# Weight halves in tiles of 1024 columns, a reordered boundary, and a gate block moved ahead in a two-layer gMLP and forgetting-attention kernel

## The chip, the cores and the metric

The kernel runs on one core of a Trainium2 chip. TensorE (PE) multiplies, VectorE (DVE) and ScalarE (ACT) do elementwise work, GpSimd (POOL) does a few small operations, and SyncE (SP) issues most transfers. Each engine runs its instructions in order; semaphores join them. The metric is the device time of one execution in microseconds; lower is better.

## The reference

A model of 1024 features over 512 tokens, with 256 memory rows. Layer A is a gMLP block with four heads of attention on the memory; layer B attends with forget gates (12 heads of 64) and again on the memory. Each layer ends in a feed-forward network of 2816 hidden columns. RMS norms stand before and behind every block:

```python
a = rmsnorm(h, ln_mix_pre[layer])
# layer A: u, v, q_mem = split(a @ w_in_a)
main = gelu(u) * (tril(w_s) @ layernorm(gelu(v)) + b_s)      # per chunk of 128 tokens, 6 groups
# layer B: q, q_mem = split(a @ w_in_b); k, v, log_f from s_in @ w_shared_kv
main = softmax(q k^T / 8 + c_t - c_s, causal) v              # c = cumsum(log_f)
mem_out = memory_attention(q_mem, mem_n, w_mem_kv)           # 4 heads of 64, 256 rows
h = h + rmsnorm(concat(main, mem_out) @ w_out, ln_mix_post)
f = rmsnorm(h, ln_ffn_pre)
h = h + rmsnorm((silu(f @ w_gate) * (f @ w_up)) @ w_down, ln_ffn_post)
```

All is in fp32.

## The kernel before

**Number form.** Every fp32 operand of a matrix product is kept as two tiles, hi and lo, of a faster type (fp32r). `split` (L240) makes them: ScalarE copies `hi`, VectorE subtracts `lo = src - hi`. `mm3` (L191 to 195) then does three products, hi times hi, hi times lo, lo times hi. So each weight goes: transfer of 512 KB to a `raw` tile (128 x 1024, four buffers, SP's queue), two splits of 512 columns, and the products. The halves lie in eight slots of 512 columns for `hi` and eight for `lo` (`pair_of_parts`, L133). In rows of the profile these are `whi<-raw` on ACT and `wlo<-raw,whi` on DVE.

**The order.** A scheduler sets each engine's order from the order of the code, from priorities (`high_priority` lets a block go first) and from explicit order constraints (`issue_after`, and `behind`, L249, which does it for several instructions). What a slot, PSUM buffer or `raw` buffer holds must be released before the next user starts.

**Layer A** (`layer_a`, L565). Tokens and query weights are loaded and multiplied first (`query_weights`, `tokens`). The input's norm ends in a sum (`st`), `var` on VectorE, a power on GpSimd (`rsqrt`, L262), and a broadcast on TensorE (`rb`, L259): `Norm.finish` (L281) is the first part, `spread` (L298) the second. The memory's norm (`var_2`, `rb_2`) goes the same way; then keys and values of the memory are made (`mem_project`) and four heads attend to it (`attend`, with `mp`, `tr`, `mo`). `fill` is a queue of pieces of value work (24: three blocks of eight), each 12 matmuls of 256 columns. `pieces(n)` puts n of them ahead of the next step, and `attend` takes the remaining sixteen between its heads. Behind the attend, `gate_inputs(m)` (L680) makes the gate columns u for one group, `stats` and `normed` the layer norm of v, and `spatial` multiplies with the spatial weights (`rows` and `s` are its products).

**The boundary** (L857) joins a block's output projection to the next block's input. `tail(tb)` (L772) ends one quarter of the tokens: it adds the product to y, squares it with a running sum on ScalarE (L793), adds the sum (L795), takes the power on GpSimd, and scales y (L814). `turn(half, pairs)` transposes y on TensorE (`yt`, L821), adds it to the residual h (L826), scales and splits the next input (`hs`, `xs`), and squares it (`nnorm.pair`, L314). `group` runs the first products of the next block while the second half is being turned; `nnorm.finish` and `spread` (rb_3 and rb_4 at the first FFN boundary) give the scale to `evac`.

**The FFN** (L1042). Gate and up products run as `Seven` (L947): a Strassen-like scheme of seven products of 12 matmuls of 256 columns on sums of weight blocks, in the order 1, 7, 2, 6, 4, 3, 5. `sums` adds the blocks in `raw` on VectorE; each product splits its own 512-column block. `end` adds the products (L1008 to L1011), and the rows are gated. In the first pair of an FFN products 1, 2, 3 of both come first. 40 Sevens run in all. The down products (`moving_pair`, `y`) stream through the same slots. `combined` (L923) makes the input's sums.

**The end.** `give` (L1329) turns, adds and stores the last tokens; the last quarter is stored in four pieces, alternating on SP's and ACT's queue.

## Time and profile before

| | |
|---|---|
| median of three runs | 1121.44 us (1121.39 to 1121.47) |
| the profiled execution | 1121.42 us |
| its span, first to last instruction | 1119.7 us |
| granted TensorE clock, mean | 0.999 |
| PE, PEld, DVE, ACT, POOL busy | 1107.3, 1002.7, 892.0, 660.3, 28.5 us |

The span leaves out 1.72 us around the first and the last instruction. A row of a timeline gives start and duration in us, engine, line, operation, output and inputs, shapes, the count of instructions put together (x), and in brackets the idle time before with what ended it. A row of a group gives busy time and the mean ns of one. A row of waits gives total, times and the longest. A row with only a time, a duration and a name is a piece of the chain of waits that ended last. Matmuls are pipelined: one of 256 columns shows 0.28 us, but the next starts before it has ended.

### The profile page before, as it was taken

How to read it: one execution, taken by the hardware profiler on the slowest of the kernel's cores; microseconds unless marked ns; L12 is line 12 of the kernel's file. 1: busy time of each engine (PE TensorE's matmuls, PEld its weight loads, DVE VectorE, ACT ScalarE, POOL GpSimd, SP SyncE). 2: the span in 40 equal slices, each digit the busy share in tenths (PEclk: the TensorE clock that was granted, in tenths of full speed). 3: DMA queues.
4: the chain of work that ended last, by engine and by line, in shares of the span. 5: the costliest groups of instructions: out<-in, count | busy, mean ns of one | idle time of the engine just before them, and what ended most of it. 6: DMA issues, size and time to landing. Idle time of an engine off the chain costs nothing.

```text
span 1119.7 us, 19536 instructions
## 1 busy us (share of the span) xinstructions
PE 1107.3 (99%) x7409; PEld 1002.7 (90%) x7409; DVE 892.0 (80%) x1721; ACT 660.3 (59%) x1388; POOL 28.5 (3%) x41
## 2 busy tenths in 40 slices
PE   8999999999999999999999999999999999999998
PEld 6998889999899899998988898889999899899996
DVE  7979448999598578796968889958998598588776
ACT  7775458755266255476757677768765266255453
POOL 0100001000000000001000000001000000000000
PEclk9999999999999999999999999999999999999999
DMA  7413231334224234244242655421235234233222
GB/s 265 151 49 109 77 97 58 100 108 151 76 89 140 74 99 127 76 135 148 63 128 59 153 128 137 135 76 57 65 106 152 74 101 133 70 109 118 76 76 76
DMA packets 63557, 118.12 MB, mean 105 GB/s; under 512 B 5164, under 2 KB 39992, under 8 KB 63464
## 3 DMA queue, kind: packets, MB, share of 16 engines
q1 hardware_dynamic: 62584, 116.05, 33.8%
q8 instruction: 58, 0.95, 0.4%
q0 software_dynamic: 192, 0.52, 0.2%
q10 hardware_dynamic: 688, 0.31, 0.1%
q14 instruction: 35, 0.29, 0.1%
HBM read 104.71 MB, written 2.10 MB: 95 GB/s over the span
## 4 chain that ended last, share of the span: by engine, by line
PE 86%; DVE 7%; ACT 3%; issue 2%; POOL 1%; DMA 1%; SPq 0%; POOLq 0%; DVEq 0%; ACTq 0%
PE y L193 9%; PE y L195 9%; PE y L194 9%; PE a L194 5%; PE a L193 5%; PE a L195 5%; PE ps L195 3%; PE ps L194 3%; PE ps L193 3%; PE e L193 3%; PE e L194 3%; PE x L194 3%; PE x L193 3%; PE x L195 3%; PE e L195 3%; DVE wlo L241 2%
## 5 line engine op out<-in xcount | busy, mean ns | idle before, releaser
L241 ACT CAST whi<-raw 128x512 fp32r<-128x512 f32 x460 | 276.2, 620 | 267.0 <-PE y L195 118.6
L241 DVE TENSOR_TENSOR wlo<-raw,whi 128x512 fp32r<-128x512 f32 x460 | 305.2, 685 | 108.8 <-ACT whi L241 106.6
L193 PE MATMUL y<-whi,fhi 128*128 128x512 f32 (+1 forms) x356 | 140.0, 394 | 0.0
L194 PE MATMUL y<-wlo,fhi 128*128 128x512 f32 (+1 forms) x356 | 139.4, 392 | 0.0
L195 PE MATMUL y<-whi,flo 128*128 128x512 f32 (+1 forms) x356 | 139.4, 392 | 0.0
L194 PE MATMUL a<-xslo,whi 128*128 128x256 f32 x320 | 90.0, 281 | 0.0
L194 PE MATMUL x<-xslo,whi 128*128 128x256 f32 x320 | 89.9, 281 | 0.0
L195 PE MATMUL x<-xshi,wlo 128*128 128x256 f32 x320 | 89.9, 281 | 0.0
L193 PE MATMUL x<-xshi,whi 128*128 128x256 f32 x320 | 89.8, 281 | 0.0
L193 PE MATMUL a<-xshi,whi 128*128 128x256 f32 x320 | 89.8, 281 | 0.0
L195 PE MATMUL a<-xshi,wlo 128*128 128x256 f32 x320 | 89.8, 281 | 0.0
L193 PEld LDWEIGHTS y<-whi,fhi 128*128 128x128 f32 x356 | 66.9, 188 | 15.7 <-ACT fhi L241 0.7
L195 PEld LDWEIGHTS y<-whi,flo 128*128 128x128 f32 x356 | 66.9, 188 | 15.5 <-DVE flo L241 0.2
L194 PEld LDWEIGHTS y<-wlo,fhi 128*128 128x128 f32 x356 | 67.0, 188 | 14.7 <-DVE wlo L241 0.2
L193 PE MATMUL ps<-xshi,whi 128*128 128x256 f32 (+1 forms) x224 | 67.5, 304 | 0.0
L195 PE MATMUL ps<-xshi,wlo 128*128 128x256 f32 (+1 forms) x224 | 67.1, 302 | 0.1
L194 PE MATMUL ps<-xslo,whi 128*128 128x256 f32 (+1 forms) x224 | 66.4, 299 | 0.0
L193 PEld LDWEIGHTS a<-xshi,whi 128*128 128x128 f32 x320 | 60.4, 189 | 0.4
L194 PEld LDWEIGHTS a<-xslo,whi 128*128 128x128 f32 x320 | 60.3, 188 | 0.3
L193 PEld LDWEIGHTS x<-xshi,whi 128*128 128x128 f32 x320 | 60.4, 189 | 0.0
L195 PEld LDWEIGHTS x<-xshi,wlo 128*128 128x128 f32 x320 | 60.3, 189 | 0.0
L194 PEld LDWEIGHTS x<-xslo,whi 128*128 128x128 f32 x320 | 60.3, 188 | 0.0
(283 smaller groups left out, 3091.1 us busy)
## 6 DMA issues: line engine op xcount, KB each, us to landing
raw<-in_w_gate SPq DMA_DIRECT2D x44, 512.0 KB, 3.6
raw<-in_w_up SPq DMA_DIRECT2D x44, 512.0 KB, 3.5
raw<-in_w_down SPq DMA_DIRECT2D x44, 512.0 KB, 4.0
raw<-in_w_out SPq DMA_DIRECT2D x16, 512.0 KB, 4.5
raw<-in_w_b_q SPq DMA_DIRECT2D x8, 512.0 KB, 3.5
raw<-in_w_a_v SPq DMA_DIRECT2D x6, 512.0 KB, 7.0
raw<-in_w_a_u SPq DMA_DIRECT2D x6, 512.0 KB
raw<-in_w_v SPq DMA_DIRECT2D x6, 512.0 KB, 3.7
```

Of the source, the lines that this page charges most:

```text
L193: PE.matmul(o, w[0], x[0], start=start, stop=False, skip_group_check=more)
L194: PE.matmul(o, w[0], x[1], start=False, stop=False, skip_group_check=more)
L195: return PE.matmul(o, w[1], x[0], start=False, stop=stop, skip_group_check=more)
L241: last_parts[:] = A.copy(hi, src), (eng or V).tensor_sub(lo, src, hi)
```

## The change

Six things change.

1. The hi and lo tiles become four slots of 1024 columns each. `columns` cuts them. Most splits stay 512 wide, within one slot; but the Sevens' pairs (1,2), (6,3) and (5,4), the gate weights `w_a_u` and the FFN's down weights in its middle groups (`whole`) are split by one instruction of 1024 columns per engine. Product 7 takes a slot by itself. In layer B a query and a key share one slot.
2. The second query weight is loaded as two halves of 256 KB; the feature blocks 1 to 3 of x are issued behind its first half.
3. In layer A twelve value pieces, formerly eight, stand ahead of the memory's projection, and its key weights are loaded later. The attend's filler is then twelve value pieces and the four pieces of a `gate_block(0)`; `gate_inputs(0)` behind the attend is gone. Its GELU goes with the values'.
4. `var` and the power in `Norm.finish` get high priority.
5. At a boundary the last quarter's square and sum (`chain`) stand ahead of the squares of the first half's turned pairs 2 and 3; the second half's squares are made behind `evac`; `combined` stands behind the last turned parts.
6. The last tail has high priority as the others do; `give_last` scales feature blocks 0 to 3 on ScalarE and adds two at a time on VectorE, turns into another PSUM tag for them, and issues all four stores on SP.

TensorE does the same matmuls as before. VectorE's rows fall from 1667 to 1475 and ScalarE's from 1262 to 1061, as the compiled order counts them with neighbours of one line and tile put together.

In the orders below a name's number tells instances apart; a row is line, operation, output and inputs, and the output's shape. The first place is VectorE at the memory norm: `mparts` are the memory's lo parts, `var` the sum plus epsilon. Before:

```order
L246 SCALAR_TENSOR_TENSOR mparts_402<-mem_329,gains,mparts_402 128x256
L246 SCALAR_TENSOR_TENSOR mparts_405<-mem_329,gains,mparts_405 128x256
L241 TENSOR_TENSOR wlo_411<-raw_408,whi_410 128x512
L241 TENSOR_TENSOR wlo_415<-raw_408,whi_414 128x512
L241 TENSOR_TENSOR wlo_421<-raw_418,whi_420 128x512
L241 TENSOR_TENSOR wlo_425<-raw_418,whi_424 128x512
L292 TENSOR_SCALAR var_433<-st_428 128x2
```

Now:

```order
L251 SCALAR_TENSOR_TENSOR mparts_420<-mem_319,gains,mparts_420 128x256
L251 SCALAR_TENSOR_TENSOR mparts_423<-mem_319,gains,mparts_423 128x256
L298 TENSOR_SCALAR var_449<-st_444 128x2
L251 SCALAR_TENSOR_TENSOR mparts_426<-mem_320,gains,mparts_426 128x256
L251 SCALAR_TENSOR_TENSOR mparts_429<-mem_320,gains,mparts_429 128x256
```

`var` has moved ahead of the weight splits and of most memory parts. TensorE has 60 matmuls between `st` and `rb` here, where 48 stood.

The second place is TensorE at the first FFN boundary, where the last quarter's y is first turned (`yt`) between products of the next block (`ps`). Before:

```order
L193 MATMUL ps_2056<-xshi_1940,whi_2036 128x256
L194 MATMUL ps_2056<-xslo_1941,whi_2036 128x256
L821 MATMUL yt_2106<-ident,y_1652 128x128
L193 MATMUL ps_2054<-xshi_1989,whi_1880 128x256
L194 MATMUL ps_2054<-xslo_1990,whi_1880 128x256
L821 MATMUL yt_2106<-ident,y_1667 128x128
```

Now:

```order
L198 MATMUL ps_1987<-xshi_1891,whi_1971 128x256
L199 MATMUL ps_1987<-xslo_1892,whi_1971 128x256
L200 MATMUL ps_1987<-xshi_1891,wlo_1972 128x256
L848 MATMUL yt_2037<-ident,y_1595 128x128
L848 MATMUL yt_2037<-ident,y_1610 128x128
```

The turns of the two quarters (y_1652 and y_1667 before, y_1595 and y_1610 now) stand together, behind 36 products since the turn before, where 26 stood.

The third place is VectorE in a steady Seven of the first FFN (`e`, `a`, `x` are its PSUM products, `s` its sums). Before:

```order
L1008 TENSOR_TENSOR s_3_2794<-e_2792,s_3_2794 128x256
L974 TENSOR_TENSOR raw_2923<-raw_2925,raw_2923 128x512
L241 TENSOR_TENSOR wlo_2959<-s_4_2932,whi_2958 128x512
L975 TENSOR_TENSOR raw_2923<-raw_2923 128x512
L241 TENSOR_TENSOR wlo_2988<-raw_2923,whi_2987 128x512
L241 TENSOR_TENSOR wlo_3005<-raw_2925,whi_3004 128x512
L1009 TENSOR_TENSOR s_3_2794<-a_2791,s_3_2794 128x256
L1011 TENSOR_TENSOR s_3_2793<-x_2790,s_3_2793 128x512
L1063 TENSOR_TENSOR s_3_2794<-s_3_2794,rbc 128x512
L1063 TENSOR_TENSOR s_3_2793<-s_3_2793,rbc 128x512
L241 TENSOR_TENSOR wlo_3021<-raw_2923,whi_3020 128x512
L241 TENSOR_TENSOR wlo_3037<-raw_2925,whi_3036 128x512
```

Now:

```order
L1013 TENSOR_TENSOR raw_2947<-raw_2947 128x512
L246 TENSOR_TENSOR wlo_2875<-raw_2814,whi_2874 128x1024
L1054 TENSOR_TENSOR s_3_2697<-a_2694,s_3_2697 128x256
L1056 TENSOR_TENSOR s_3_2696<-x_2693,s_3_2696 128x512
L1108 TENSOR_TENSOR s_3_2697<-s_3_2697,rbc 128x512
L1108 TENSOR_TENSOR s_3_2696<-s_3_2696,rbc 128x512
L246 TENSOR_TENSOR wlo_2892<-raw_2816,whi_2891 128x1024
```

Two splits of 512 around the last sums have become one of 1024 ahead of them, for (6,3), and one behind them, for (5,4).

The diff, cut to its core:

```diff
--- before.py
+++ after.py
@@ -130,11 +130,12 @@
-    def pair_of_parts(n=512, aside=False):
-        if aside:
-            return act("whi"), act("wlo")
-        return (wp.tile([P, max(n, 512)], F32R, tag="hi", name=name("whi"), bufs=8)[:, :n],
-                wp.tile([P, max(n, 512)], F32R, tag="lo", name=name("wlo"), bufs=8)[:, :n])
+    def pair_of_parts(n=1024):
...
+        return [wp.tile([P, max(n, 1024)], F32R, tag=t, name=name(f"w{t}"), bufs=4)[:, :n] for t in ("hi", "lo")]
...
+    def columns(pair, c0, c1):
+        return [t[:, c0:c1] for t in pair]
@@ -146,32 +147,36 @@
-    def prepared(src, shape, eng=None):
+    def prepared(src, shape, step=512):
...
-        return weight_parts(raw, shape, eng)
...
-    def weight_parts(raw, shape, eng=None):
+        return weight_parts(raw, shape, step)
...
+    def weight_parts(raw, shape, step=512):
...
-        parts = []
-        for d in range(0, n, 512):
-            pair = pair_of_parts(min(512, n - d))
-            split(raw[:, d : min(d + 512, n)], *pair, eng)
-            parts += cut(pair, shape[1])
-        return parts
...
-    def moving_pair(src, aside=False):
+        pair = pair_of_parts(n)
+        for c in range(0, n, step):
+            at = c, min(c + step, n)
+            split(raw[:, at[0] : at[1]], *columns(pair, *at))
+        return cut(pair, shape[1])
...
+    def moving_pair(src, aside=False, whole=False):
...
+        pair = [] if aside else pair_of_parts()
+        if whole:
+            split(four, *(t.rearrange("p (k m c) -> p m k c", m=4, k=2) for t in pair))
...
-            hi, lo = (t.rearrange("p (m c) -> p m c", m=4) for t in pair_of_parts(aside=aside))
-            split(four[:, :, x, :], hi, lo)
+            both = (act("whi"), act("wlo")) if aside else columns(pair, 512 * x, 512 * x + 512)
+            hi, lo = (t.rearrange("p (m c) -> p m c", m=4) for t in both)
+            if not whole:
+                split(four[:, :, x, :], hi, lo)
@@ -289,8 +294,9 @@
-            V.tensor_scalar_add(v[:, t0:t1], st[:, t0:t1], RMS_EPS)
-            rsqrt(self.r4[:, t0:t1], v[:, t0:t1], t1 - t0)
+            with tc.high_priority():
+                V.tensor_scalar_add(v[:, t0:t1], st[:, t0:t1], RMS_EPS)
+                rsqrt(self.r4[:, t0:t1], v[:, t0:t1], t1 - t0)
@@ -582,10 +588,12 @@
-        query_weights(1, 0, 1024)
-        tokens(1, 2)
-        tokens(2, 4)
+        query_weights(1, 0, 512)
+        with tc.issue_after(last_load[0].ins):
+            tokens(1, 2)
+            tokens(2, 4)
...
+        query_weights(1, 512, 1024)
@@ -620,7 +628,27 @@
-            fill = queue([value_block(j) for j in range(3)])
+            us, wu = [], []
...
+            def gate_block(m):
...
+                o = []
...
+                def load():
+                    wu.append(prepared(i["w_a_u"][m], (KT, P), 1024))
...
+                def piece(n):
+                    if n == 0:
+                        o.append(ps("mm", s="u"))
+                    for k in range(2 * n, 2 * n + 2):
+                        mm3(o[0], wu[m][k], a[k], k == 0, k == KT - 1)
+                    if n == 3:
+                        us.append(plain("u"))
+                        V.tensor_mul(us[m], o[0], rbc)
...
+                return load, [lambda n=n: piece(n) for n in range(4)]
...
+            fill = queue([value_block(j) for j in range(3)] + [gate_block(0)])
@@ -645,11 +673,11 @@
-            pieces(1)
+            pieces(3)
...
+            norm.finish((0, NMEM))
...
-            norm.finish((0, NMEM))
-            pieces(3)
+            pieces(5)
@@ -659,7 +687,7 @@
-                for vt in vg.values():
+                for vt in (*vg.values(), us[0]):
@@ -721,7 +747,6 @@
-            gate_inputs(0)
@@ -765,7 +790,7 @@
-            return tc.high_priority() if tb == TB - 1 and not last else ExitStack()
+            return tc.high_priority() if tb == TB - 1 else ExitStack()
@@ -881,7 +908,12 @@
-                nnorm.pair(j, cols)
+                if sums:
+                    nnorm.pair(j, cols)
...
+        def second_turn():
+            turn(1, range(2, 4), False)
+            turned_parts.extend(last_parts)
@@ -896,14 +929,19 @@
-        tail(3, lambda: turn(0, (2,)))
-        turn(0, (3,))
+        tail(3, lambda: turn(0, (2,), False))
+        with behind(chain):
+            nnorm.pair(2, h0)
+        turn(0, (3,), False)
+        with behind(chain):
+            nnorm.pair(3, h0)
...
-                     after={3: lambda: turn(1, range(2)), 5: lambda: turn(1, range(2, 4)),
-                            6: lambda: nnorm.finish(h0)})
+                     after={3: lambda: turn(1, range(2), False), 5: second_turn, 6: lambda: nnorm.finish(h0)})
...
+        for j in range(KT // 2):
+            nnorm.pair(j, h1)
@@ -952,54 +990,61 @@
-            w1, w2 = loaded(src(0)), loaded(src(1))
-            self.a = [w[:, d : d + 512] for w in (w1, w2) for d in (0, 512)]
+            self.raws = loaded(src(0)), loaded(src(1))
+            self.a = [w[:, d : d + 512] for w in self.raws for d in (0, 512)]
...
-        def parts(self, src):
-            pair = pair_of_parts()
+            self.w = {}
...
+        def parts(self, src, *which):
+            n = 512 * len(which)
+            pair = pair_of_parts(n)
...
-            return pair
+            for x, n in enumerate(which):
+                self.w[n] = columns(pair, 512 * x, 512 * x + 512)
...
-            self.w1 = self.parts(a11)
+            self.parts(self.raws[0], 1, 2)
...
-            self.w2 = self.parts(a12)
...
-            for k, w in enumerate(cut(w, P)):
+            for k, w in enumerate(cut(self.w[w], P)):
...
-            a11, a12, a21, a22 = self.a
...
+            if what in (3, 6) and 3 not in self.w:
+                self.parts(self.raws[0], 6, 3)
+            elif what in (4, 5) and 4 not in self.w:
+                self.parts(self.raws[1], 5, 4)
+            elif what == 7:
+                self.parts(self.s3, 7)
...
-                self.product(self.p, self.w1, 0)
+                self.product(self.p, 1, 0)
...
-                self.product(self.x[:, left], self.w2, 2)
+                self.product(self.x[:, left], 2, 2)
...
-                self.product(self.x[:, right], self.parts(a12), 5)
+                self.product(self.x[:, right], 3, 5)
...
-                self.product(self.q, self.parts(a22), 4, True)
+                self.product(self.q, 4, 4, True)
...
-                self.product(self.p, self.parts(a21), 6, True)
+                self.product(self.p, 5, 6, True)
...
-                self.product(self.p, self.parts(a11), 3, True)
+                self.product(self.p, 6, 3, True)
...
-                self.product(self.q, self.parts(self.s3), 1)
+                self.product(self.q, 7, 1)
@@ -1081,10 +1126,11 @@
-        a, close = boundary(phase, G_MIX_POST + layer, G_FFN_PRE + layer, nnorm, rb, first, evac_first, scaled)
+        a, close, turned_parts = boundary(phase, G_MIX_POST + layer, G_FFN_PRE + layer, nnorm, rb, first, evac_first, scaled)
...
-        xs, last = combined(a, scaled, xp)
+        with behind(turned_parts):
+            xs, last = combined(a, scaled, xp)
@@ -1117,7 +1163,7 @@
-                    w = down_weights(layer, k0 + 2 * kp, dh)
+                    w = down_weights(layer, k0 + 2 * kp, dh, whole=True)
@@ -1265,7 +1310,8 @@
-            pair["q"], pair["k"] = pair_of_parts(), pair_of_parts()
+            both = pair_of_parts()
+            pair["q"], pair["k"] = columns(both, 0, 512), columns(both, 512, 1024)
@@ -1326,17 +1372,35 @@
-    def give(tb, order, queues=(nc.sync,)):
+    def give_last(tb):
...
+        c0, c1 = tb * P, (tb + 1) * P
+        at = slice(c0, c1)
+        for k0, k1 in ((4, 6), (0, 2), (6, 8), (2, 4)):
+            tr = ps("tr" if k0 >= 4 else "mm", s="yt")
+            for x, k in enumerate(range(k0, k1)):
+                turned(ys, k, (tb,), tr[:, x * P : (x + 1) * P])
+            if k0 >= 4:
+                for x, k in enumerate(range(k0, k1)):
+                    residual(tr[:, x * P : (x + 1) * P], k, (c0, c1), G_FFN_POST + 1)
+            else:
+                t = temp("g", (P, 2, P))
+                for x, k in enumerate(range(k0, k1)):
+                    A.activation(t[:, x, :], tr[:, x * P : (x + 1) * P], AF.Copy, scale=gain(G_FFN_POST + 1, k))
+                V.tensor_add(h[:, k0:k1, at], h[:, k0:k1, at], t)
+            nc.sync.dma_start(out[:, k0:k1, at], h[:, k0:k1, at])
...
+    def give(tb, order):
...
-        for n, some in enumerate(order):
+        for some in order:
...
-            queues[n % len(queues)].dma_start(out[:, k0:k1, c[0] : c[1]], h[:, k0:k1, c[0] : c[1]])
+            nc.sync.dma_start(out[:, k0:k1, c[0] : c[1]], h[:, k0:k1, c[0] : c[1]])
```

41 lines of the change are left out of this document (21 added, 20 removed).

## The prediction, made before the changed kernel was run

> **What bounds the kernel now.** I read the page first, then what TensorE waits for, then the stretches of time, and at last the timelines around each wait.
>
> ```profile
> span 1119.7 us, 19536 instructions
> PE 1107.3 (99%) x7409; PEld 1002.7 (90%) x7409; DVE 892.0 (80%) x1721; ACT 660.3 (59%) x1388; POOL 28.5 (3%) x41
> ...
> PE rb L259 <- POOL r L262: 2.5, 4, 1.7
> PE yt L821 <- ACT y L814: 1.0, 2, 0.5
> PE ps L193 <- ACT whi L241: 0.7, 1, 0.7
> PE e L193 <- ACT s L1003: 0.4, 1, 0.4
> PE tr L456 <- DVE mp L449: 0.3, 1, 0.3
> ```
>
> TensorE is busy 99% of the span, and the change takes no matrix product away. So its time can only come out of TensorE's waits: 1119.7 - 1107.3 = 12.4 us, ramp and final transfer among them. The list (total, times, longest) says where: the broadcasts of a norm (rb) for a GpSimd power, the turning of y (yt) for ScalarE, and single waits at the start, in the FFN (e) and in attention (tr). VectorE's 80% is an average over unlike stages:
>
> ```profile
> 30.00:60.00 30.00, 27.95 (x233) 27.43 (x233) 26.18 (x58) 21.83 (x52) 3.81 (x2) 1.00 0.47 150
> 160.00:195.00 35.00, 34.31 (x245) 31.57 (x244) 26.82 (x57) 28.81 (x60) 3.80 (x5) 1.00 0.13 39
> 245.00:265.00 20.00, 20.00 (x171) 20.00 (x170) 20.00 (x36) 12.71 (x28) 0.00 (x0) 1.00 0.36 109
> ```
>
> The columns are the stretch, its length, and the busy time of PE, PEld, DVE, ACT, POOL. Layer A has 2.05 us of PE gap in 30; the first boundary 0.69 in 35. In the first FFN's gate and up products VectorE is full, 20.00 of 20, while TensorE is not held up: that cover is thin.
>
> **The first loads.** The second query weight, 512 KB, is first needed at 7.5 us:
>
> ```profile
> 1.75 5.72 DMA raw<-in_w_a_q
> 8.17 0.49 PE L193 MATMUL ps<-ahi,whi 128*128 128x512 f32 x1 [0.69 <-ACT whi L241]
> raw<-in_w_a_q SPq DMA_DIRECT2D x2, 256.0 KB, 3.2
> ```
>
> The 256 KB load issued at 0.81 landed after 3.2 us, at 4.0; 768 KB more (a block of x and this weight) came by 7.47, 3.46 us later. Split in halves, the first leaves 256 KB behind it: 3.46 x 256/768 = 1.15 us earlier. TensorE's wait at 8.17 (0.69, and two idle matmuls in front) goes; the blocks of x that now come later could hold the next steps. I take -0.9, bounds 0 and -1.2.
>
> **The memory norm (var_2, rb_2).** The largest wait:
>
> ```profile
> 31.86 2.49 DVE L241 TENSOR_TENSOR wlo<-raw,whi 128x512 fp32r<-128x512 f32 x4
> 34.27 0.15 DVE L292 TENSOR_SCALAR var<-st 128x2 f32<-128x2 f32 x1
> 34.34 2.48 DVE L241 TENSOR_TENSOR wlo<-raw,whi 128x512 fp32r<-128x512 f32 x4
> 34.49 2.89 POOL L262 TENSOR_TENSOR r<-var,mhalf 128x2 f32<-128x2 f32 x1 [7.56 <-DVE var L292]
> 34.25 0.28 PE L194 MATMUL ps<-mparts,whi 128*128 128x256 f32 x1
> ...
> 35.44 0.28 PE L195 MATMUL ps<-mparts,wlo 128*128 128x256 f32 x1
> 37.44 0.43 PE L259 MATMUL rb<-ident,r 128*128 128x128 f32 x2 [1.73 <-POOL r L262]
> ```
>
> The sum stands on VectorE behind memory parts and four weight splits; the power then takes 2.89 us, beside four more splits (VectorE instructions with two SBUF inputs), though one of this size takes 0.98 elsewhere (187.18 below). The matmul after 35.44 would have started at 35.56, so 1.88 us are lost. After the change var follows two memory parts, and 60 matmuls at 0.119 (34.25 to 35.44 is ten of them) stand between the sums and rb_2, 7.1 us, where 48 stood. The twelve more come from value pieces, which are moved ahead; the memory's key weights go behind the value weights on SP's queue for it, and nothing asks for them before rb_2. Even a power of 2.89 us and a var 1.5 us late fit in. I take -1.9; bounds -1.9 and -0.9 (if half of that lateness is left).
>
> The rest of layer A: the wait on mp (0.3 in the list) loses the splits beside it, but the mem_v split now waits for a 1024-wide slot that the memory products free. I take -0.2, bounds -0.5 and +0.3. The filler of the attend keeps its sixteen pieces of 12 x 0.119 = 1.4 us (a gate piece is six matmuls of 512, as long). But `gate_inputs(0)`, 5.6 us, stood behind the attend and hid GELU, statistics and the normalised v:
>
> ```profile
> 80.03 1.03 PE L456 MATMUL tr<-ident,mp 128*128 128x128 f32 x8
> 89.40 1.31 POOL L262 TENSOR_TENSOR rv<-rv,mhalf 128x4 f32<-128x4 f32 x1 [42.75 <-DVE rv L694]
> 94.45 0.68 DVE L241 TENSOR_TENSOR vlo<-vg,vhi 128x512 fp32r<-128x512 f32 x1
> 100.56 0.27 PE L738 MATMUL rows<-wlo,tri 128*128 128x128 f32 x1
> ```
>
> The spatial products begin behind the last of `rows`, at 100.7; without those 5.6 us at 95.1, and the second vlo is ready at 95.13. The spatial weights' splits now lie ahead, in the attend, and bring that some 1 us earlier. It just fits: +0.3, bounds 0 and +1.0.
>
> **The two FFN boundaries (yt_5, rb_3).**
>
> ```profile
> 174.14 0.61 ACT L241 CAST whi<-raw 128x512 fp32r<-128x512 f32 x1
> 175.40 1.34 ACT L814 ACTIVATE y<-y,r 128x512 f32<-128x512 f32 x2 [0.64 <-POOL r L262]
> 176.17 0.76 PE L821 MATMUL yt<-ident,y 128*128 128x128 f32 x5 [0.51 <-ACT y L814]
> 763.33 1.34 ACT L814 ACTIVATE y<-y,r 128x512 f32<-128x512 f32 x2 [0.64 <-POOL r L262]
> 186.86 0.15 DVE L292 TENSOR_SCALAR var<-st 128x2 f32<-128x2 f32 x1
> 187.18 0.98 POOL L262 TENSOR_TENSOR r<-var,mhalf 128x2 f32<-128x2 f32 x1 [11.82 <-DVE var L292]
> 188.22 0.43 PE L259 MATMUL rb<-ident,r 128*128 128x128 f32 x2 [0.18 <-POOL r L262]
> ```
>
> TensorE stands 0.51 us (0.8 with the broken pitch around it) until y is scaled, at both boundaries. Now 36 products of 256 columns stand between yt_4 and yt_5 instead of 26: ten times 0.119 = 1.2 us more cover, and the chain is no later. The wait goes. Against it, one product's split (wlo) now lies one 512-wide row (0.69) later on VectorE, half of it uncovered by my reading of the order, 0.3. And rb_3 has 8 products behind its sums, not 23. They ended at 188.2 - 23 x 0.119 = 185.5, so var, at 186.86, was 1.4 us late on VectorE. High priority takes that away and 15 x 0.119 = 1.8 of cover goes: +0.4, or nothing if var now comes at once; I take 0. Each boundary -0.8 + 0.3 + 0.0 = -0.5, bounds -0.8 and +0.4, so -1.0 for two. The boundary in front of layer B has the same exchange with smaller waits: -0.2, bounds -0.5 and +0.5.
>
> **The 1024-wide splits.** No row has one. From
>
> ```profile
> L241 DVE TENSOR_TENSOR wlo<-raw,whi 128x512 fp32r<-128x512 f32 x460 | 305.2, 685 | 108.8 <-ACT whi L241 106.6
> L1009 DVE TENSOR_TENSOR s<-a,s 128x256 f32<-128x256 f32 x40 | 16.7, 417 | 2.8 <-ACT s L997 2.7
> 219.12 3.09 DVE L241 TENSOR_TENSOR wlo<-raw,whi 128x512 fp32r<-128x512 f32 x5
> 261.53 1.14 ACT L241 CAST whi<-raw 128x512 fp32r<-128x512 f32 x2
> ```
>
> 256 columns take 0.417 and 512 take 0.685; so 1024, an estimate, 0.685 + 2 x 0.268 = 1.22, bounds 0.685 and 1.37 (once and twice the 512). Five in a row take 3.09, a pitch of (3.09 - 0.685)/4 = 0.60; at such a pitch a 1024 takes 0.60 + 2 x 0.268 = 1.13, so a merged pair saves VectorE 0.07. A gate-up pair of Sevens lasts 14 products of 12 matmuls, 14 x 12 x 0.119 = 19.9 us. VectorE's rows in it were 30 of 512 and 4 of 256 (0.33 apart), 19.3 us; now they are 6 of 1024, 18 of 512 and 4 of 256: 6.8 + 10.8 + 1.3 = 18.9. This is worth the wait at 266 (e on s, 0.4 in the list and 0.2 around it) and nothing more: TensorE is full in the steady Sevens. -0.6, bounds 0 and -0.7.
>
> The price is coarser slots. A Seven now takes all four; each comes free after the second of its two products and is needed again four products later (4 x 1.42 = 5.7 us). ScalarE's half (two of its 512s take 1.14, last row above) and VectorE's 1.13 leave 3.4 us. For the pair (5,4) VectorE has the last sums of the Seven before in front (0.3 + 3 x 0.60, behind a copy of 0.4): 0.4 + 2.1 + 1.1 = 3.6, which leaves 2.1. In the first Sevens of each FFN those sums come on top of `combined`, which now stands behind the turned parts, and the third product waits for a 1024-wide split in place of a 512-wide one. VectorE's rows from the last broadcast to that split are 8.6 us long by the order and these durations, 7.1 before: 1.5 more is the upper bound of a new wait there, and a 1024-wide split's extra length, 1.13 - 0.69 = 0.4, the lower. I take 0.5, since TensorE has the products with hi to do first; twice: +1.0.
>
> **Tail.**
>
> ```profile
> 1113.66 2.75 DVE L826 SCALAR_TENSOR_TENSOR h<-yt,gains,h 128x128 f32<-128x128 f32 x9
> 1115.24 1.58 ACTq L1339 DMA_DIRECT2D out<-h  x2
> 1114.03 2.19 SPq L1339 DMA_DIRECT2D out<-h  x3
> ```
>
> VectorE's nine updates (0.31 apart) end at 1116.4 and the last transfer follows. Four of them become four scalings on ScalarE and two sums of 256 (0.33 apart): two 0.31 saved, and the turns no longer wait for `tr` slots. All four transfers queue on SP, 0.4 apart, which gives part back. -0.4, bounds 0 and -0.6.
>
> Sum: -0.9 - 1.9 - 0.2 + 0.3 - 1.0 - 0.2 - 0.6 + 1.0 - 0.4 = -3.9. Attention in layer B keeps its products; where its query and key pair share one slot I count 0, bounds -0.5 and +1.0. The profiled run's own time is 1121.42 (1.72 more than its span), 0.02 under the median: 1121.4 - 3.9 = **1117.5 us**.
>
> **Rivals.** *The FFNs take it back.* The first Sevens' waits come at 1.5 each, boundaries give nothing, and the wait at 266 stays (VectorE full, 20.00 of 20, speaks for it): -0.9 - 1.9 - 0.2 + 0.3 + 3.0 - 0.4 = -0.1, or 1121.3 at the worst; halfway to the forecast, 1119.4, is its lower end, and 1120.4 its middle. *Slower: VectorE becomes the bound in the Sevens.* If a 1024-wide split holds VectorE for twice a 512's duration, 1.37, six per gate-up pair add 6 x 0.24 = 1.4 to 18.9: 20.3 of 19.9 us. Each of the 20 pairs (40 Sevens) would lose 0.4, +8, about 1125.5. It decides from 1.30 a split ((19.9 - 18.9)/6 + 1.13). The row of 256 against 512 speaks against it, since the slope would have to change. The Trainium skill, "VectorE: DVE Perf Modes", section "The TRN2 errata — SBUF-src ops pay a fixed extra latency per instruction", says that one large tile pays the gap once and many small ones each time; by that rule a merged pair is cheaper, as I took it. *A slow power at the boundaries.* With 8 to 12 products of cover, a power of 2.89 in place of 0.98 at rb_3 and its two likes costs 3 x 1.9 = 5.7, about 1123.2. For it speaks 34.49 above; against it, that only one full-size split stands beside var there, not four. The Trainium skill, "GPSIMD Engine Reference", section "8. Key points", says that GpSimd shares its SBUF interfaces with VectorE and suffers from instructions with two SBUF inputs; the two rows agree. *The change doesn't do what it says*: the order that is compiled leaves every wait where it is, 1121.4. Little speaks for it, since var_2's new place is read from the order itself.
>
> **How the numbers follow.** The forecast has a chance of 0.66, the FFN rival 0.17, VectorE's bound 0.08, the slow power 0.06, no change 0.03. This kernel's measurements tell 0.2% (2.24 us) from no change. Under 1119.2 lie nearly all of the forecast and a sixth of the FFN rival: 0.69. Over 1123.7 lie VectorE's bound and part of the slow power: 0.11. The rest, 0.20, is within. The terms' lower bounds add to -1.2 - 1.9 - 0.5 - 1.6 - 0.5 - 0.7 - 0.6 - 0.5 = -7.5, and the first Sevens' +0.8 makes -6.7; not all come together, so the range begins at -6.4, 1115.0. Its upper end takes in most of the FFN rival, 1120.9.
>
> **What would show it.** rb_2 without a wait on the power; no wait of yt on y at 175 and 763; the query wait at 8 gone; a 1024-wide split near 1.22; in the Sevens no wait of TensorE on wlo or whi. Waits of e or x on a split in every Seven, or rb waits over 1.5 us at the boundaries, would prove me wrong.

## The result, and the profile after

The changed kernel takes 1127.55 us (median; 1126.25 to 1128.53), the kernel before beside it 1121.45: a ratio of 1.0054, 95% interval 1.0041 to 1.0067. It is slower, by 6 us. The forecast was 1117.5, the range 1115.0 to 1120.9, and slower had a chance of 0.11. Times are medians, since a single execution can stray: one of ten of a kernel in the experiments (all splits 512 wide) took 1807.35 us.

The profiled execution took 1126.25 us. Its page begins:

```profile
span 1124.5 us, 19060 instructions
PE 1103.8 (98%) x7408; PEld 998.5 (89%) x7409; DVE 882.3 (78%) x1559; ACT 640.0 (57%) x1232; POOL 28.5 (3%) x41
```

VectorE (DVE) and ScalarE (ACT) have 10 and 20 us less to do than before, and TensorE (PE) is busy 3.5 us less for the same products. The span is nevertheless 4.8 us longer, so TensorE's idle time went from 12.4 to 20.7 us. The list of TensorE's waits (total, times, longest) says for whom:

```profile
PE e L200 <- DVE wlo L246: 2.8, 3, 1.4
PE ps L198 <- ACT whi L246: 2.8, 4, 1.0
PE x L198 <- ACT whi L246: 2.2, 2, 1.1
PE a L198 <- ACT whi L246: 1.6, 4, 0.6
PE rb L264 <- POOL r L267: 1.3, 3, 0.6
...
PE yt L848 <- ACT y L841: 1.1, 2, 0.6
```

The rb wait of 1.7 us is gone from the list, as forecast. New or longer are waits of the Sevens (`e`, `x`, `a`) and of the boundary products (`ps`, 0.80 at each FFN boundary) for split weights. The yt wait, which was to go, stands there as before, and so does the wait for the second query weight: it is 1.02 of the 2.8 us on `ps`, now at 7.06 (before, 0.69 at 8.17). Where the time went is read from the start times of the same products in both traces (kernel after minus kernel before, in us):

| stretch | forecast | measured |
|---|---|---|
| start to the first turning of y (layer A) | -2.7 | -2.80 |
| the two FFN boundaries (first turning of y to the first Seven) | -1.0 | +1.04 and +1.10 |
| first group of each FFN (its first Seven to the first Seven of the next group) | +1.0 | +3.13 and +4.85 |
| the other groups of the first FFN, without its last Sevens | -0.6 for both FFNs | -1.33 |
| the last Sevens of the first FFN | | +1.28 |
| the other groups of the second FFN | | -1.68 |
| boundary before layer B | -0.2 | +0.20 |
| attention of layer B | 0 | -1.11 |
| tail | -0.4 | +0.16 |
| sum | -3.9 | +4.84 |

Three kinds of stretches made the kernel slower: the FFN boundaries, the last Sevens of the first FFN, and above all the first group of each FFN. Here are three stretches of 10 us from the first Seven of the first FFN, before and then after (stretch, length, busy time of PE, PEld, DVE, ACT, POOL, then clock, DMA share and GB/s):

```profile
210.46:220.46 10.00, 10.00 (x86) 10.00 (x85) 8.95 (x18) 7.33 (x15) 0.00 (x0) 1.00 0.07 16
220.46:230.46 10.00, 10.00 (x87) 10.00 (x86) 8.00 (x14) 5.39 (x13) 0.00 (x0) 1.00 0.57 196
230.46:240.46 10.00, 10.00 (x86) 10.00 (x86) 9.98 (x19) 5.39 (x12) 0.00 (x0) 1.00 0.34 107
```

```profile
208.70:218.70 10.00, 8.69 (x69) 8.08 (x68) 8.13 (x14) 4.98 (x8) 0.00 (x0) 1.00 0.31 99
218.70:228.70 10.00, 10.00 (x86) 10.00 (x87) 7.56 (x11) 5.27 (x10) 0.00 (x0) 1.00 0.44 144
228.70:238.70 10.00, 9.00 (x72) 8.40 (x71) 9.97 (x17) 6.69 (x12) 0.00 (x0) 1.00 0.11 26
```

TensorE was never short there; now it loses 1.3 and 1.0 us. VectorE does less in the first two stretches (8.13 and 7.56 of 10) and is full in the third, where TensorE waits. It was not too slow on average; it could not work ahead.

The timeline of that place shows what held it (start, duration, engine; idle time before and its releaser in brackets):

```profile
221.29 0.28 PE L199 MATMUL e<-t3lo,whi 128*128 128x256 f32 x1
221.61 1.05 ACT L246 CAST whi<-raw 128x1024 fp32r<-128x1024 f32 x1 [2.58 <-PE e L199]
222.63 0.69 DVE L1011 TENSOR_TENSOR s<-raw,raw 128x512 f32<-128x512 f32 x1 [2.44 <-DMA raw<-in_w_gate]
223.24 3.49 DVE L246 TENSOR_TENSOR wlo<-raw,whi 128x1024 fp32r<-128x1024 f32 x3
227.58 0.68 DVE L1014 TENSOR_TENSOR raw<-raw,raw 128x512 f32<-128x512 f32 x1
229.71 1.28 DVE L1108 TENSOR_TENSOR s<-s,rbc 128x512 f32<-128x512 f32 x2
233.50 0.69 DVE L1015 TENSOR_TENSOR raw<-raw 128x512 f32<-128x512 f32 x1
234.41 2.94 ACT L246 CAST whi<-raw 128x1024 fp32r<-128x1024 f32 x3
```

ScalarE's cast at 221.61 waits for a product (`e`): no slot is free until TensorE has read one. The `e` that ends just before it is product 7 (its input is `t3`), which holds a whole slot with half of its columns. Then three splits come in one piece at 223.24, two for the first two Sevens and one for the third, and the third Seven's sums fall behind them and behind the end of the two Sevens before. The last of those sums runs at 233.50, the cast that reads it starts at 234.41, behind ScalarE's casts of rows, and TensorE waits at 235.5 to 237.2.

At the boundary, the profile shows the power of y's last quarter (before, it took 0.92 us, from 174.44, and y was scaled at 175.40):

```profile
171.10 0.21 DVE L820 SCALAR_TENSOR_TENSOR v<-ss,rms_eps 128x1 f32<-128x1 f32 x1
171.23 0.68 DVE L246 TENSOR_TENSOR wlo<-raw,whi 128x512 fp32r<-128x512 f32 x1
171.39 2.13 POOL L267 TENSOR_TENSOR r<-v,mhalf 128x1 f32<-128x1 f32 x1 [7.26 <-DVE v L820]
171.83 0.68 DVE L246 TENSOR_TENSOR xslo<-hs,xshi 128x512 fp32r<-128x512 f32 x1
172.43 0.68 DVE L326 TENSOR_TENSOR sq<-sq,sq 128x512 f32<-128x512 f32 x1
173.55 1.33 ACT L841 ACTIVATE y<-y,r 128x512 f32<-128x512 f32 x2 [1.58 <-POOL r L267]
177.29 0.39 PE L198 MATMUL ps<-xshi,whi 128*128 128x256 f32 x1 [0.80 <-ACT whi L246]
```

Counted from the first turning of y (161.60 now, 164.40 before), `v` comes at 9.50 us, 0.25 earlier than before (9.75), but the power takes 2.13 us beside three full-size VectorE instructions. So y is scaled at 11.95, where it was 11.00: 0.95 us later, nearly all of the boundary's +1.04. ScalarE stands idle for 1.58 us in front of that, the next weight casts come behind it, and a boundary product waits for one at 177.29.

### The profile page after: what moved, and what is told of

It reads as the page before. It is cut to its first block, busy times and chain, and to the rows that moved or that the text cites. A ratio compares the mean times of both kernels' runs of the same rounds, so it can differ in the third digit from the quotient of the medians.

```text
span 1124.5 us, 19060 instructions
## 1 busy us (share of the span) xinstructions
PE 1103.8 (98%) x7408; PEld 998.5 (89%) x7409; DVE 882.3 (78%) x1559; ACT 640.0 (57%) x1232; POOL 28.5 (3%) x41
## 4 chain that ended last, share of the span: by engine, by line
PE 84%; DVE 8%; ACT 4%; issue 2%; DMA 1%; POOL 1%; SPq 0%; POOLq 0%; DVEq 0%
PE y L198 9%; PE y L200 9%; PE y L199 9%; PE a L200 4%; PE a L198 4%; PE a L199 4%; PE ps L200 3%; PE ps L199 3%; PE ps L198 3%; PE e L200 3%; PE x L200 3%; PE x L198 3%; PE x L199 3%; PE e L198 3%; PE e L199 3%; DVE wlo L246 2%
## 5 line engine op out<-in xcount | busy, mean ns | idle before, releaser
L246 ACT CAST whi<-raw 128x1024 fp32r<-128x1024 f32 (+1 forms) x302 | 247.6, 844 | 260.5 <-PE y L200 97.5
L246 DVE TENSOR_TENSOR wlo<-raw,whi 128x1024 fp32r<-128x1024 f32 (+1 forms) x302 | 286.5, 969 | 96.0 <-ACT whi L246 94.0
L200 PEld LDWEIGHTS a<-xshi,wlo 128*128 128x128 f32 x320 | 60.4, 189 | 0.0
```

Source lines behind the costliest of these rows:

```text
L200: return PE.matmul(o, w[1], x[0], start=False, stop=stop, skip_group_check=more)
L246: last_parts[:] = A.copy(hi, src), (eng or V).tensor_sub(lo, src, hi)
```

## Experiments

Times are medians beside runs of the kernel before on the same chip; "first groups" are the two first groups of the table. Line numbers differ from kernel to kernel.

**The parts one by one.** The changes of layer A alone, on the kernel before (512-wide slots, old boundary, old end; the norm's sum with high priority stays in):

```diff
-            V.tensor_scalar_add(v[:, t0:t1], st[:, t0:t1], RMS_EPS)
-            rsqrt(self.r4[:, t0:t1], v[:, t0:t1], t1 - t0)
+            with tc.high_priority():
+                V.tensor_scalar_add(v[:, t0:t1], st[:, t0:t1], RMS_EPS)
+                rsqrt(self.r4[:, t0:t1], v[:, t0:t1], t1 - t0)
...
-            pieces(1)
+            pieces(3)
             xs = mem_inputs(0, memt)
-            wk = mem_key_weights(0)
             norm.finish((0, NMEM))
-            pieces(3)
+            wk = mem_key_weights(0)
+            pieces(5)
```

> The kernel before with parts 2, 3 and 4 of the change alone (halved query load, twelve value pieces ahead and the gate block in the attend, high priority for var and the power); slots of 512, old Sevens, old boundary order, old end. Theory L (layer A's gain is real and needs none of the tiles): the start and the memory norm give -2.8 us as in the changed kernel's trace up to the first yt, so 1118.6, and S1 (the first product of the first Seven) comes some 2.8 us earlier than before. Rival (the gain hangs on the four 1024-wide slots): about 1121, yt no earlier. If the priority of var alone disturbs the boundaries, up to +1 on top.

Measured: 1118.28 against 1121.27, ratio 0.9975 (0.9965 to 0.9984). Layer A ends 2.62 us earlier, and each FFN boundary is about 0.5 us shorter (45.43 us for the first, 46.05 before): of these changes only the high priority touches them. So layer A's gain is real and needs no wider tiles.

The tiles alone, on the kernel before:

```diff
-        return (wp.tile([P, max(n, 512)], F32R, tag="hi", name=name("whi"), bufs=8)[:, :n],
-                wp.tile([P, max(n, 512)], F32R, tag="lo", name=name("wlo"), bufs=8)[:, :n])
+        return [wp.tile([P, max(n, 1024)], F32R, tag=t, name=name(f"w{t}"), bufs=4)[:, :n] for t in ("hi", "lo")]
```

> The kernel before with part 1 alone: four slots of 1024 columns, and the 1024-wide splits in the Sevens, the gate weights and the down weights. Theory T (the tiles alone make the FFNs wait, by merged splits or by coarse slots): the first gate-up group of each FFN loses 3 to 5 us and the group ahead of the last down products of the first FFN 1.3, the steady groups gain some 3 us in all: 1121.4 + 9.5 - 3 = 1128, at least 1126. Theory B (the boundary's new order fills VectorE ahead of the first Sevens, and the tiles alone are harmless): 1118 to 1121, no wait of x or e on a split over 0.5 us.

Measured: 1127.85, ratio 1.0062 (1.0045 to 1.0079). The first groups lose 2.4 and 3.8 us, the last Sevens of the first FFN 1.4, and attention gains 0.8. The tiles alone cost as much as the whole change.

The changed kernel with the old boundary (the squares back in their turns, `combined` not held):

```diff
-        tail(3, lambda: turn(0, (2,), False))
-        with behind(chain):
-            nnorm.pair(2, h0)
-        turn(0, (3,), False)
-        with behind(chain):
-            nnorm.pair(3, h0)
+        tail(3, lambda: turn(0, (2,)))
+        turn(0, (3,))
...
-        with behind(turned_parts):
-            xs, last = combined(a, scaled, xp)
+        xs, last = combined(a, scaled, xp)
```

> The changed kernel with part 5 undone: squares at the boundary where they were, combined not held behind the turned parts, no chain constraint; the tiles, layer A and the end as changed. Theory B: the first Sevens' waits go with it, -6 to -10 us, 1118 to 1121. Theories M and S: only the boundaries' own loss comes back, 1.0 at each FFN boundary, 1125 to 1126; the waits of product 3 in the first Seven, 1.3 each, stay.

Measured: 1122.77, ratio 1.0010 (1.0001 to 1.0020). The boundaries are short again (45.53 us for the first), the first groups lose 2.2 and 5.2. The time lies between the two forecasts. So the tiles alone cost 6.6 us, layer A alone brings 3.0, and the new boundary costs 4.9 on top of both (1.0054 against 1.0010). The first two don't simply add: 6.6 - 3.0 = 3.6, and this run, with the new end besides, is 1.5 us slower than the kernel before. That was not followed.

**Slot or instruction?** The wide tiles change two things: a split is one instruction of 1024, and a slot comes free only when both its products are done. First, the changed kernel with the Sevens' splits 512 wide and made when needed, in the same 1024-wide slots:

```diff
-            if what in (3, 6) and 3 not in self.w:
-                self.parts(self.raws[0], 6, 3)
-            elif what in (4, 5) and 4 not in self.w:
-                self.parts(self.raws[1], 5, 4)
+            if what in (3, 6):
+                self.half(what, (6, 3))
+            elif what in (4, 5):
+                self.half(what, (5, 4))
```

> The changed kernel with one thing undone: in the Sevens each product's weight is split by itself, 512 columns wide, when its own inputs are there; the four shared slots of 1024 stay, and so do all other parts. Theory M (a merged split waits for the later of its two inputs and takes twice as long): the waits of x, a and e on whi and wlo go, -6 to -8 us, 1120 to 1121.5. Theory S (four coarse slots are what is missing): the waits stay, 1126 to 1128. Theory B (the boundary's order): 1126 to 1128 too, with the waits at the first product 3.

Measured: 1124.47, ratio 1.0029 (1.0017 to 1.0040). About half of the loss comes back, which again lies between the forecasts. In the profiled execution, 2.1 us above the median, the first groups still lose 3.2 and 4.8 us. The waits in the Sevens are gone, and the loss stands at the groups' end, in the first down products:

```profile
PE y L198 <- DVE s L1060: 4.9, 2, 2.6
```

Then all splits of the FFN 512 wide, the down weights too (`down_weights(layer, k0 + 2 * kp, dh)` without `whole=True`):

> The changed kernel with all splits of the FFNs 512 wide, in the Sevens when each product's own input is there, and in the down products; the four shared slots of 1024 stay. In the run with narrow Sevens the loss had moved to the first down products, where ScalarE's last copy stood behind two 1024-wide casts of down weights that waited for slots. Theory M: nothing is left of the loss, +0.5 us a group at most, 1117 to 1119. Theory S: +2 to +4 us a group remain, at whatever place, 1123 to 1126.

Measured: 1122.14 against 1121.81, ratio 1.0010 (1.0000 to 1.0019). By the ratios 4.9 us of the change's 6.1 come back (1.0054 - 1.0010, on two chips). The profiled execution, at 1125.51, is 3.4 us above the median; its first groups lose 2.8 and 2.3 us, in the first FFN most of it in a wait of 2.2 us in the first down products. What the other executions lose there was not seen.

Last, the instructions stay wide and only the slots change: product 7, a 512-wide split that takes a whole 1024-wide slot in the change, gets a slot of its own (two plain buffers fewer make room):

```diff
-            pair = pair_of_parts(n)
+            pair = pair_of_parts(n) if n > 512 else [wp.tile([P, 512], F32R, tag=f"{t}7", name=name(f"w{t}"), bufs=1) for t in ("hi", "lo")]
```

> The changed kernel, but product 7 of a Seven has a slot of 512 columns of its own, so the three merged pairs of a Seven rotate over four slots instead of sharing them with product 7; paid for by two plain buffers less (10 for 12); splits stay merged. The orders are the same up to the first product 7. Theory S (few coarse slots keep VectorE from splitting the next Seven's weights ahead of the sums that end the first pair): from the first product of an FFN's Sevens to the end of its first group's down products the changed kernel lost 3.1 and 4.9 us; half of it or more comes back, 1122 to 1124. Theory M (the merged instruction itself, which waits for the later of two inputs and lasts 1.22 us): nothing comes back, 1127 to 1128.

Measured: 1121.47 against 1121.81, ratio 0.9997 (0.9988 to 1.0007): again by the ratios, 6.4 us come back. The first groups lose 0.5 and 1.4, and the last Sevens of the first FFN nothing. So the long instruction does no harm where a slot is to be had. And since narrow instructions bring most of it back in the coarse slots, by the medians the slots alone do little harm either: it takes both. What the narrow kernel's profile still loses in the first groups, the new boundary costs with slots of 512 too (next). Where product 7 takes one of the four wide slots, a Seven uses all four and little of the next can be split ahead; when slots do come free, the splits come as long ones in a lump.

**What in the boundary costs?** Layer A's changes with the new boundary, without the tiles (the boundary lines of the front's diff, on the first experiment):

> Parts 2, 3, 4 and 5 without the tiles and the new end: the run with layer A alone, and the boundary's new order. Theory P (the new order puts three VectorE splits and sums beside the last quarter's power, which takes 2.13 us for 0.92, and ScalarE's weight casts behind the scaling): from the first turn to the first Seven the boundary loses 1.0 us more than in the run with layer A alone at each FFN boundary and up to 1.5 in front of layer B, 1121 to 1122. Rival (the loss at the boundaries comes from the slots of 1024): 1118.3, no loss, and the power under 1.2 us.

Measured: 1125.47, ratio 1.0033 (1.0020 to 1.0046), 6.5 us above layer A alone and above both forecasts. The first FFN boundary takes 47.12 us (46.05 before), the second is about 1.25 us longer than before, both with a power of 2.13 us. The first groups lose 4.3 and 1.7, now in the first down products:

```profile
PE y L193 <- DVE s L1042: 2.9, 2, 2.3
```

The same without the hold of `combined` (`with behind(()):` for `with behind(turned_parts):`):

> Layer A and the new boundary without tiles (the run before this one of that kind: +4.4 us in the first FFN's first group, against +0.1 with the old boundary), but combined no longer held behind the turned parts. Theory H (the hold puts VectorE's sums of the input, about 1.3 us more VectorE work, behind the first Seven, and the first group has no room for it): the first group's loss falls under 1.5 us, 1121.5 to 1123. Rival Q (the squares of the second half, moved behind evac, do it): the loss stays over 3 us, 1125.

Measured: 1124.75, ratio 1.0027 (1.0017 to 1.0037). The first groups still lose 3.8 and 1.2 us. The hold is worth nothing that can be told.

The same with the hold, but the squares of pairs 2 and 3 back in their turns, ahead of the last quarter's sum:

```diff
-        tail(3, lambda: turn(0, (2,), False))
-        with behind(chain):
-            nnorm.pair(2, h0)
-        turn(0, (3,), False)
-        with behind(chain):
-            nnorm.pair(3, h0)
+        tail(3, lambda: turn(0, (2,)))
+        turn(0, (3,))
```

> Layer A and the new boundary without tiles, but the squares of pairs 2 and 3 of the first half back inside their turns and no longer behind the last quarter's chain. Theory P (they were what kept VectorE's splits and sums away from the last quarter's power): the power at the first and second FFN boundary falls from 2.13 to under 1.2 us and TensorE comes 0.8 to 1.2 us earlier from the last first-half turn to the first second-half turn at each boundary, 1123 to 1124. Rival (the tail's own place is the cause, the squares are not): the power stays at 2.13 and the time at 1125.

Measured: 1118.41, ratio 0.9976 (0.9965 to 0.9986). All of the loss is gone, at the boundaries (45.45 us) and in the first groups (-0.2 and +0.1). The timeline of its boundary:

```profile
172.29 0.62 ACT L241 CAST whi<-raw 128x512 fp32r<-128x512 f32 x1
172.30 0.21 DVE L815 SCALAR_TENSOR_TENSOR v<-ss,rms_eps 128x1 f32<-128x1 f32 x1
172.43 0.68 DVE L241 TENSOR_TENSOR xslo<-hs,xshi 128x512 fp32r<-128x512 f32 x1
172.59 0.92 POOL L262 TENSOR_TENSOR r<-v,mhalf 128x1 f32<-128x1 f32 x1 [7.52 <-DVE v L815]
173.55 1.34 ACT L836 ACTIVATE y<-y,r 128x512 f32<-128x512 f32 x2 [0.64 <-POOL r L262]
```

Here y is first turned at 162.56, in the changed kernel at 161.60, so the equal 173.55 are not the same moment of the boundary. Counted from that turning, `v` comes 0.24 us later here (9.74 for 9.50), the power is 1.2 us shorter, and y is scaled at 10.99, not 11.95: 0.96 us earlier. The new order wins a quarter of a microsecond for `v` and loses five times that in the power. In both rows the power ends 0.4 us behind 173.11, the end of the full-size VectorE instructions with two SBUF inputs that run beside it from its start (here `xslo` alone, there three in a row), as if it waited them out. The three weight casts behind the scaling move with it: they start 14.06 us behind the turning here and 15.02 there.

**Is there room on VectorE?** Four additions of 512 columns that nobody reads (4 x 0.60 = 2.4 us) at the first Sevens of the first FFN, on layer A's changes alone. The second FFN has none and is the control:

```diff
+        if layer == 0:
+            dead = temp("dead")
+            for _ in range(4):
+                V.tensor_add(dead, rbc, rbc)
```

> The run with layer A alone, and four additions of 512 columns on VectorE, 2.4 us in all, whose result nobody reads, placed with the first sums of the first FFN's Sevens (the second FFN is left as it was, as a control). Theory V (VectorE has no room in an FFN's first group, so work added at its start is paid by TensorE before the group ends): the first FFN loses 1.5 to 3 us from its first Seven to the end of its first down products, the second FFN nothing: 1120 to 1121. Rival (VectorE's gaps of 2 to 3 us in the first 20 us of the Sevens take it in): under 0.5 us, 1118.3 to 1118.8.

Measured: 1123.29, ratio 1.0017 (1.0008 to 1.0027), 4.7 us above the same kernel without them and above both forecasts. In the profiled execution the first group of the first FFN loses 3.4 us, that of the second 0.2. The wait is again in its first down products, and one in the Sevens:

```profile
PE y L193 <- DVE s L1029: 1.9, 1, 1.9
PE x L193 <- ACT whi L241: 1.0, 1, 1.0
```

Work of VectorE that lands at that place costs its whole length and more; without it the same group loses 0.1 us.

**The tail.** The last four stores alternately on SP's and ScalarE's queue (`(nc.sync, nc.scalar)[n % 2].dma_start`), one execution:

> The changed kernel with the last four stores alternating on SP's and ACT's queue as before the change. From the start of the last power to the end of the span it took 6.63 us before the change and 7.35 in the changed kernel's profile. Theory Q (four issues on SP, 0.5 us apart, end last): 0.4 to 0.6 us shorter. Rival (the landing of the last store sets the end): no difference over 0.15 us.

Measured: 1128.62. From the start of the last power to the end it takes 7.25 us, in the change 7.35 and before 7.16 (the 6.63 in the expectation is counted from the power's end). So the queue is about 0.1 of it, as the rival said, in one execution of each. In the change, VectorE's part:

```profile
1117.19 0.54 POOL L267 TENSOR_TENSOR r<-v,mhalf 128x1 f32<-128x1 f32 x1 [6.27 <-DVE v L820]
1119.55 2.02 SPq L1391 DMA_DIRECT2D out<-h  x4
1120.29 0.42 DVE L1390 TENSOR_TENSOR h<-h,g 128x256 f32<-128x256 f32 x1
```

VectorE is done 3.52 us after the power's start (1120.71); before, its nine updates ended at 1116.41, 3.86 after the power's start at 1112.55. The 0.34 us were gained there, and from there to the end it took 3.83 us instead of 3.30, of which 0.4 pass before the last store is issued (1121.14).

**The version that follows.** Tiles and layer A of the change, product 7 in its own slot, the old boundary (its lines as in the run above) and the old end:

```diff
-            pair = pair_of_parts(n)
+            pair = pair_of_parts(n) if n > 512 else [wp.tile([P, 512], F32R, tag=f"{t}7", name=name(f"w{t}"), bufs=1) for t in ("hi", "lo")]
...
-    give_last(TB - 1)
+    give(TB - 1, (range(4, 6), range(2), range(6, 8), range(2, 4)), (nc.sync, nc.scalar))
```

> The changed kernel's tiles and layer A with the boundary's old order and the old end, and product 7 in a slot of its own (10 plain buffers). Theory S, with the boundary's loss separate from it: up to the first Seven as in the run with layer A alone (-3.2 us against before), first groups -0.2 to +0.8 each where the changed kernel lost 3.1 and 4.9, steady groups and the place at 492 another -0.5 to -1.5: 1116.5 to 1118.0, the fastest so far. Rival (the two losses are one: whatever order the tiles meet, the first groups lose 2 us or more): 1120 to 1122.

Measured: 1116.63 against 1121.25, ratio 0.9959 (0.9947 to 0.9972): faster than both kernels. Its first groups lose 0.2 and 0.0 us. The first stretches of its first FFN and the timeline there:

```profile
207.21:217.21 10.00, 9.95 (x82) 9.69 (x81) 8.01 (x13) 5.81 (x9) 0.00 (x0) 1.00 0.17 52
217.21:227.21 10.00, 10.00 (x87) 10.00 (x86) 9.30 (x13) 5.96 (x10) 0.00 (x0) 1.00 0.46 159
```

```profile
215.43 2.36 DVE L246 TENSOR_TENSOR wlo<-raw,whi 128x1024 fp32r<-128x1024 f32 x2 [1.41 <-ACT whi L246]
218.39 1.22 DVE L246 TENSOR_TENSOR wlo<-raw,whi 128x1024 fp32r<-128x1024 f32 x1
220.16 1.22 DVE L246 TENSOR_TENSOR wlo<-raw,whi 128x1024 fp32r<-128x1024 f32 x1 [0.54 <-ACT whi L246]
224.27 0.68 DVE L1002 TENSOR_TENSOR raw<-raw 128x512 f32<-128x512 f32 x1
```

In the second stretch VectorE works 9.30 us, not 7.56: the splits that came in one piece at 223.24 are done before, and the last sum of the third Seven runs at 224.27, 17.1 us behind the first Seven's start, not 24.8 (233.50 - 208.70). In the kernel before it ran 18.1 us behind it.

Four kernels now differ in the slot of product 7 and in the boundary (and this one in the end, worth under 0.2 us). By the ratios the own slot is worth 6.4 us with the new boundary (1.0054 against 0.9997) and 5.7 with the old (1.0010 against 0.9959); the old boundary is worth 4.9 us in shared slots and 4.3 with the own slot. So these are two losses that add, 10.7 us together (1.0054 against 0.9959), and the rest of the change gains 4.6.

## Why the prediction was wrong, step by step

**What held.** Layer A: -2.7 forecast, -2.80 measured. The power of the memory norm takes 0.89 us (2.89 before), rb_2 no longer waits for it, and the spatial products lost nothing, where I had taken +0.3: from the first value piece on, layer A gained 2.0 us in the profiled execution where the terms made 1.8. The -0.9 for the first loads is not shown, and part of the -2.80 may be chance: the first value piece, behind the query weights, starts 0.80 us earlier in this execution (19.01, before 19.81), but in the twelve profiled kernels with the new loads between 18.62 and 20.85, with a mean of 19.7. The query wait that was to go is still there (1.02 us at 7.06). The 1024-wide split was sized right: 1.22 us by the estimate and by the groups of the changed kernel, which rules out the rival that VectorE becomes the bound by a longer split.

```profile
L246 DVE TENSOR_TENSOR wlo<-raw,whi 128x1024 fp32r<-128x1024 f32 x158 | 191.5, 1223 | 84.9 <-ACT whi L246 83.6
L246 ACT CAST whi<-raw 128x1024 fp32r<-128x1024 f32 x158 | 164.8, 1049 | 227.5 <-PE y L200 96.0 <-PE x L199 52.2 <-DVE raw L1015 32.9
```

The Trainium skill, "VectorE: DVE Perf Modes", section "The TRN2 errata — SBUF-src ops pay a fixed extra latency per instruction", says that a single large tile pays the gap between instructions once and many small ones each time. The trace agrees: 1.22 us for the wide one, 2 x 0.69 for two narrow ones. In a row the gain is small: three wide ones take 3.49 us (223.24 above), a pitch of 1.14 where two narrow ones take 1.20. The kernel is slower all the same.

**The step that failed: "The price is coarser slots".** It said that a Seven takes all four slots, reckoned 3.4 and 2.1 us of slack in the steady Sevens, and put +0.5, at most 1.5, on each first group, for one product's split. The steady Sevens bore the slack out (-1.33 and -1.68, where -0.6 was forecast for both FFNs). The first groups lost 3.13 and 4.85. The step looked at one wait, product 3's, and that is there, 1.3 us with the new boundary. It did not ask what full slots do to the work ahead. Before, the last splits of the first two Sevens were done at 222.2 (the five from 219.12 in the prediction), 11.7 us behind the first Seven's start. Now they wait for a product (221.61 above) and come in a lump with the third Seven's first, done at 226.7, 18.0 us behind it. That pushes the third Seven's sums into the stretch where VectorE is full (9.97 of 10, and 9.98 in the kernel before). The own slot takes the cause away, narrow instructions most of the lump. The last Sevens of the first FFN, +1.28, were not in the sum at all; the own slot takes them away too.

**The second failed step: "The wait goes" at the FFN boundaries.** Forecast -0.5 each, measured +1.04 and +1.10. More products do stand in front of the turn that waited, though eight and not ten: 36 where 28 stood (26, and two behind the other quarter's turn), 0.95 us of cover. But "the chain is no later" is true only of `v`, which is 0.25 us earlier. Three VectorE instructions with two SBUF inputs now run beside the power, which takes 2.13 us for 0.92. So y is scaled 0.95 us later, counted from its first turning: the cover is eaten, and the wait of 0.51 stays. The mechanism is that of the rival *a slow power at the boundaries*, but at the power of y's last quarter; at rb_3, where I had looked for it, the power takes 0.99. The Trainium skill, "GPSIMD Engine Reference", section "8. Key points", names that contention, between GpSimd and VectorE instructions with two SBUF inputs. The rows here agree and put 0.92 and 2.13 us on it. That the new place of the two squares is the cause, of the boundary's loss and of the boundary's share in the first groups, is shown with slots of 512 by putting them back (0.9976 against 1.0033, nothing else changed); with the wide tiles only the whole old boundary was tried (4.9 and 4.3 us). That the lengthening is the three instructions' doing is read from the rows beside it and not tried alone. How a late y costs the first group's end two to four microseconds more with slots of 512 was not followed.

**Smaller terms.** The tail's -0.4 was gained on VectorE (0.34) and given back in the stores (0.53). The wait at 266 is gone from the list, as forecast, but its group lost more elsewhere. Attention gained 1.11 us where 0 was taken, beyond my lower bound of -0.5: all kernels with wide tiles have it (-0.8 to -1.2), none without; the waits in it were 0.4 us and I did not follow it further. Why the other groups gained 3.0 in all where I took 0.6 is open too. (The prediction's product 14 x 12 x 0.119 is 20.0, not 19.9; nothing hangs on it.)

**The rivals.** *The FFNs take it back* was the right one in kind and place, with a chance of 0.17. It priced the first groups at 1.5 each, from one split's delay, and the boundaries at nothing; with 3.13, 4.85 and +2.1 it would have said slower.

## What to carry to other kernels

Count slots not only for the products that read them, but for the work that is done ahead while they are held: one 512-wide piece in a 1024-wide slot cost about 6 us (5.7 and 6.4), as much as the whole change lost, though each split had become cheaper. Before moving work of a busy engine behind a point, look whether that engine is full just after it; here 2.4 us of dead work cost 3.4. An order constraint that makes an input of GpSimd early gains nothing if it puts the VectorE instructions it displaced beside the GpSimd instruction; here 0.25 us were won and 1.2 lost. And before two traces are compared by their times, count both from the same piece of work.

## What the runs showed of the hardware

- The same power of one column takes 0.54 to 0.93 or 2.13 us on GpSimd, and one of two columns 0.70 to 2.89. The longest stand beside three and more full-size VectorE instructions with two SBUF inputs in a row; this was read from the rows and not tried alone.
- One store after another on SP's queue was issued about 0.5 us apart (1119.55, then 1120.1, 1120.6 and 1121.1); a second queue beside it gained 0.1 us (7.25 for 7.35) in one execution.
- With the same first loads, in twelve kernels, the first value piece starts anywhere from 18.62 to 20.85 us, so a term of 0.9 us there can't be read from one execution of each kernel.
